# Undivided attention maps, moved sample steps, a written VectorE order in the projections and a shifted output end in a hybrid GLA and differential-attention step

## The chip, the cores and the metric

One core of one Trainium2 chip runs the whole step in a single launch. The metric is device time in microseconds (us) from the first to the last instruction and what lies around them. The times of before are 1455.91, 1458.81 and 1461.02 us; their median is 1458.81 us.

## The reference, cut to what matters

1024 prompt frames and 32 sample frames of width 1024 pass one layer: an input normalisation, one large input projection, a gated linear attention (GLA) branch, a differential attention branch, two output projections that are merged by sigmoid gates, an output projection with its own normalisation, and the residual. In the differential branch each head has two attention maps; they are subtracted, and the result is normalised per head and gated:

```python
p = jax.nn.softmax(s, axis=-1)
attn = p[:, :, 0] - lam * p[:, :, 1]
o = jnp.einsum('bhqk,bkhe->bqhe', attn, v.astype(F32))
...
yg = rmsnorm(o_gla, gla_norm_g) * silu(gg)
yd = rmsnorm(o_diff, diff_subln_g) * (1.0 - lambda_init) * silu(dg)
merged = sigmoid(ma) * (yg @ w_proj_gla) + sigmoid(mb) * (yd @ w_proj_diff)
return x + rmsnorm(merged @ w_out, post_norm_g)
```

where `rmsnorm(x, g)` is `x * rsqrt(mean(x * x) + EPS) * g`. The sample frames attend to 512 cached key and value rows and to themselves.

## The kernel before, in words

All matmuls run in float32 split into a high and a low part; a product takes three matmuls (high by high, high by low, low by high), and every split of a tile is a copy on ScalarE (ACT, the high part) and a difference on VectorE (DVE, the low part). TensorE is called PE, GpSimd POOL; SP issues most DMAs, in order.

The program has these stages, by the trace's time: normalisation and value projection to about 185 us; GLA to about 545; differential attention to about 1165; the GLA branch's output projection to about 1260; the other branch's projection to about 1360; the output projection in four quarters of 256 columns to 1448.4, and the end to 1458.4.

**The order on PE.** In the attention stage a planner, class `Order`, writes PE's order. Several threads yield steps, each with a cost, the events it needs with a latency behind each, and the PSUM banks it takes; the planner keeps a clock of its own and picks the first step that is ready. The latencies stand in table `W`. Wherever the attention thread is not ready, the thread `fill` puts in matmuls of the input projection (`ps_w`, L515 to L517). The order on DVE, ACT and POOL is left to the scheduler of the language there. The PSUM banks are two of 512 columns ("pj") and two of 1024 ("s"), one of 512 for transposes ("t") and one for outputs ("o").

**The attention stage.** For each of eight heads `diff_main` goes through eight blocks i of 128 queries. `diff_scores` computes both maps' scores (`ps_s`), their negative maxima (L941) and exponentials with row sums (L943); then the reciprocal of both sums (L946), the second map scaled by its reciprocal and minus lambda (L947, w columns wide), and the first map scaled and added to it (L948). `diff_main` transposes the result in fours into the t bank (`ps_t`, L997), splits it (L999, L1000), and multiplies it by the values (`po`). `split` leaves the rotated queries and keys of even heads in four parts of two early tiles, y2 and y3, of odd heads in tiles of their own; `load_y` fills the early tiles y0 to y3 with GLA outputs at the end of head 7 (L959 to L961).

**The sample heads.** `sample_thread` takes two heads at a time: scores against cache and new rows (`ps_ss`), softmax, transposes of the probabilities in two pieces (`ps_st`, 4 and 1 blocks of columns) each put together by ACT and DVE (L1073, L1074), the product with the values (`po_s`, L1084), a normalisation, and a transpose of the output (`ps_so`, L1095) into the t bank, read by two DVE instructions (L1098). The new value rows come into `vsm`, a part of tile `smp`.

**The projections.** `pg_first` runs GLA projection jobs 0 and 1 together, `pg_job` jobs 2 to 7; each has three chunks of 352 columns, 24 matmuls each, in two "pj" banks, and each chunk is evacuated by DVE (L1147). Beside them the eight attention outputs are loaded (`ydr`, L1130), multiplied on DVE by the inverse root of their mean square (`rsb`, L1206, two heads per load, one buffer), and split into `Y` (L1133, L1134). The next projection (L491 to L493) needs all eight. While a job runs, ACT and POOL split the next weights (L481, L483).

**The end.** For each quarter u of the columns and each of nine row blocks i (the ninth is the sample block) the product is squared and summed (L1270), scaled (L1271), and in the last quarter finished row block by row block: sum (L1276), inverse root (L183, and a power on POOL, L184), two halves of 512 columns scaled and added to the rows of x (L1279), and stored (L1281). The sample block is last in every quarter.

## Time and profile before

| | before |
|---|---|
| median of three runs | 1458.81 us |
| the profiled execution's own time | 1460.14 us |
| its span, first to last instruction | 1458.4 us |
| mean granted clock of TensorE | 0.991 |
| PE busy (matmul) | 1401.2 us, 96% |
| PE weight load, beside it | 1293.0 us, 89% |
| DVE busy | 748.8 us, 51% |
| ACT busy | 555.3 us, 38% |
| POOL busy | 297.9 us, 20% |

Busy times are summed over the instructions of an engine. The matmuls of a sequence overlap each other, so the difference between the span and PE's busy time, 57 us, is only roughly what PE waits; the waits are listed by instruction in a view of their own, and the granted clock is shown by slices of time.

### The profile page before, as it was taken

What the parts mean: (1) busy time and instruction counts of PE and PEld (TensorE: products, weight loads), DVE (VectorE), ACT (ScalarE), POOL (GpSimd) and SP (SyncE); (2) the same over time, 40 slices, a digit from 0 to 9 for tenths busy, and PEclk for the clock granted to TensorE, in tenths of its full rate; (3) what the DMA queues carried; (4) which work ended last, traced back from release to release, by engine and by line L of the source; (5) the groups of instructions that cost most, each with busy time, mean ns of one, the idle gap of its engine ahead of it and who ended that gap; (6) DMA issues with size and microseconds to landing.
All of it is one profiled execution on the core that took longest, in us unless ns stands there. A gap on an engine that the chain in (4) does not pass through costs nothing.

```text
span 1458.4 us, 22595 instructions
## 1 busy us (share of the span) xinstructions
PE 1401.2 (96%) x9072; PEld 1293.0 (89%) x9072; DVE 748.8 (51%) x1440; ACT 555.3 (38%) x1154; POOL 297.9 (20%) x194
## 2 busy tenths in 40 slices
PE   8999999999999999999999999999999999999997
PEld 6687789889989899998999898988888899999996
DVE  5622005656565342656575657656775425554425
ACT  4423104535354232545444444444444332221311
POOL 1200002222223123222222221222231112221001
PEclk9999999999999999999999999999999999999999
DMA  8522111122222233213122211221232188543416
GB/s 291 171 103 89 50 46 56 46 71 92 81 64 85 75 113 103 72 54 107 50 76 78 78 64 63 77 64 51 76 115 81 60 300 313 190 142 117 151 38 224
DMA packets 64803, 152.36 MB, mean 104 GB/s; under 512 B 9584, under 2 KB 28176, under 8 KB 63152
## 3 DMA queue, kind: packets, MB, share of 16 engines
q1 hardware_dynamic: 64688, 150.80, 31.2%
q8 instruction: 75, 1.23, 0.3%
q14 instruction: 40, 0.33, 0.1%
HBM read 108.57 MB, written 40.04 MB: 102 GB/s over the span
## 4 chain that ended last, share of the span: by engine, by line
PE 47%; DVE 9%; DMA 4%; ACT 3%; issue 2%; POOL 1%; SPq 0%; DVEq 0%; POOLq 0%; ACTq 0%
PE ps_w L515 9%; PE ps_w L516 8%; PE ps_w L517 8%; PE ps_s L937 4%; PE ps_t L997 2%; PE ps_w L492 2%; PE ps_w L491 2%; PE ps_w L493 2%; DVE nm L941 2%; DMA ydr<-ydd 1%; DMA cwr<-wout 1%; PE po L1011 1%; DVE p L947 1%; PE po L1012 1%; ACT p L943 1%
## 5 line engine op out<-in xcount | busy, mean ns | idle before, releaser
L515 PE MATMUL ps_w<-X,wh 128*128 128x352 f32 x1344 | 451.8, 336 | 2.3 <-DVE sg L530 1.6
L516 PE MATMUL ps_w<-X,wl 128*128 128x352 f32 x1344 | 436.8, 325 | 0.6 <-issue 0.6
L517 PE MATMUL ps_w<-X,wh 128*128 128x352 f32 x1344 | 434.8, 324 | 0.0
L483 POOL TENSOR_TENSOR wl<-wr,wh 128x1024 fp32r<-128x1024 f32 x72 | 176.1, 2446 | 624.2 <-ACT wh L481 548.7
L515 PEld LDWEIGHTS ps_w<-X,wh 128*128 128x128 f32 x1344 | 254.0, 189 | 9.9 <-issue 4.5
L516 PEld LDWEIGHTS ps_w<-X,wl 128*128 128x128 f32 x1344 | 254.5, 189 | 0.9 <-issue 0.9
L517 PEld LDWEIGHTS ps_w<-X,wh 128*128 128x128 f32 x1344 | 253.9, 189 | 0.0
L943 ACT ACTIVATE p<-ps_s,nm 128x256 f32<-128x256 f32 (+7 forms) x128 | 94.4, 740 | 70.7 <-DVE nm L941 70.4
L327 PE MATMUL ps_v<-wh,X 128*128 128x512 f32 x248 | 97.6, 394 | 1.8 <-DVE X L243 1.8
L326 PE MATMUL ps_v<-wh,X 128*128 128x512 f32 x248 | 99.1, 400 | 0.0
L328 PE MATMUL ps_v<-wl,X 128*128 128x512 f32 x248 | 98.4, 397 | 0.0
L481 ACT ACTIVATE wh<-wr 128x1024 fp32r<-128x1024 f32 x72 | 75.9, 1054 | 53.2 <-PE ps_w L517 30.3
L941 DVE TENSOR_REDUCE nm<-ps_s 128x1 f32<-128x256 f32 (+7 forms) x128 | 93.0, 752 | 0.0
L999 ACT ACTIVATE ah<-ps_t 128x512 fp32r<-128x512 f32 (+2 forms) x96 | 47.1, 490 | 70.3 <-PE ps_t L997 69.8
L1000 DVE TENSOR_TENSOR al<-ps_t,ah 128x512 fp32r<-128x512 f32 (+2 forms) x96 | 53.1, 553 | 25.4 <-ACT ah L999 24.3
L1015 DVE SCALAR_TENSOR_TENSOR osb<-po,gs_half,sg 128x256 f32<-128x256 f32 x32 | 15.4, 483 | 92.9 <-ACT sqo L1014 92.9
L492 PE MATMUL ps_w<-Y,wl 128*128 128x352 f32 x192 | 62.2, 324 | 0.0
L491 PE MATMUL ps_w<-Y,wh 128*128 128x352 f32 x192 | 62.0, 323 | 0.0
L493 PE MATMUL ps_w<-Y,wh 128*128 128x352 f32 x192 | 61.9, 322 | 0.0
L306 ACT ACTIVATE vo<-ps_v 128x512 f32<-128x512 f32 x32 | 19.1, 595 | 106.6 <-PE ps_v L328 106.1
L997 PE MATMUL ps_t<-ident,p 128*128 128x128 f32 x288 | 49.7, 282 | 9.8 <-DVE smp L1098 7.6
L327 PEld LDWEIGHTS ps_v<-wh,X 128*128 128x128 f32 x248 | 46.7, 188 | 13.6 <-DVE X L243 2.7
(316 smaller groups left out, 2713.9 us busy)
## 6 DMA issues: line engine op xcount, KB each, us to landing
wr<-w SPq DMA_DIRECT2D x72, 512.0 KB
thd<-gate SPq DMA_DIRECT2D x16, 528.0 KB
xn<-xn SPq DMA_DIRECT2D x16, 512.0 KB
wr<-wv SPq DMA_DIRECT2D x16, 512.0 KB
newk<-pair SPq DMA_DIRECT2D x8, 528.0 KB
y<-ygd SPq DMA_DIRECT2D x8, 528.0 KB
tha<-thd SPq DMA_DIRECT2D x8, 528.0 KB
ydr<-ydd SPq DMA_DIRECT2D x8, 528.0 KB
```

Source lines behind the costliest of these rows:

```text
L326: mm(ps, xk[:, 0, t0 : t0 + P], wh[:, k, :], start=(k == 0), stop=False)
L327: mm(ps, xk[:, 1, t0 : t0 + P], wh[:, k, :], start=False, stop=False)
L328: mm(ps, xk[:, 0, t0 : t0 + P], wl[:, k, :], start=False, stop=(k == KT - 1))
L483: nc.gpsimd.tensor_tensor(wl, wr, wh.bitcast(F32), op=ALU.subtract)
L491: mm(ps[:, :n], wh[:, k, :], src[k][:, 0, t0 : t0 + n], start=(k == 0), stop=False)
L492: mm(ps[:, :n], wl[:, k, :], src[k][:, 0, t0 : t0 + n], start=False, stop=False)
L493: mm(ps[:, :n], wh[:, k, :], src[k][:, 1, t0 : t0 + n], start=False, stop=(k == KT - 1))
L515: mm(ps[:, :n], wh[:, k, :], src[k][:, 0, t0 : t0 + n], start=(k == 0), stop=False)
L516: mm(ps[:, :n], wl[:, k, :], src[k][:, 0, t0 : t0 + n], start=False, stop=False)
L517: mm(ps[:, :n], wh[:, k, :], src[k][:, 1, t0 : t0 + n], start=False, stop=(k == KT - 1))
L941: ve.tensor_reduce(nm, ps[:, 0:w], axis=AX.X, op=ALU.max, negate=True)
L943: act(p[:, 0:w], ps[:, 0:w], AF.Exp, bias=nm, accum_out=sm[:, m : m + 1])
```

## The change

Five parts:

1. **Undivided maps.** The first map is no longer divided by its row sum. The sums of the first map go into 32 columns of `smp` (`den`, one column per head and block); the second map's reciprocal, times the first map's sum and minus lambda, is made on one column, and one instruction adds the second map, so scaled, to the first. The result is larger by the first map's sum, which the later normalisation takes out; for that, EPS is multiplied by the square of the sums: after heads 3 and 7 `den` is transposed (`ps_d`), squared on ACT with scale EPS, stored, and added to the mean squares before the root, which now works on 64 by 128 values.
2. **Early tiles.** The odd heads' splits take y2 and y3 instead of the even heads'; y0 and y1 are loaded first; the early tiles are split in three parts each.
3. **Sample heads.** New value rows are loaded with the keys; the output transpose takes the o bank; the planner's latencies `sp` and `so_t` are 8.6 instead of 7.1 and 2.9 instead of 0.72; the square's unused output goes elsewhere.
4. **Merge in fixed order.** The scaling and splitting of the attention outputs is called behind projection jobs 3 to 7, and DVE's order is as written there.
5. **Shifted end.** The sample block is taken last, fifth, fifth and second in the four quarters; the finishing of a row block is put behind the evacuation of the next one; the rows of x and the raw weights of the first quarter are loaded into other buffers; in the last quarter DVE's order is as written; the last half's store is issued by ACT.

The core of the diff:

```diff
-    "sp": 7.1, "st_t": 1.14, "sv": 3.44, "spt": 0.43, "so_o": 3.58, "so": 4.1, "so_t": 0.72, "yg0": 0.0,
+    "sp": 8.6, "st_t": 1.14, "sv": 3.44, "spt": 0.43, "so_o": 3.58, "so": 4.1, "so_t": 2.9, "yg0": 0.0,
...
-        hi, lo = (even[t] if h % 2 == 0 and t in even else dp.tile([P, NP], F32R, tag=f"{t}{h % 2}", name=t)
+        hi, lo = (odds[t] if h % 2 else dp.tile([P, NP], F32R, tag=f"{t}0", name=t)
...
-            act(p[:, 0:w], ps[:, 0:w], AF.Exp, bias=nm, accum_out=sm[:, m : m + 1])
+            act(p[:, 0:w], ps[:, 0:w], AF.Exp, bias=nm, accum_out=sums[m])
...
         ve.reciprocal(sm, sm)
-        ve.tensor_scalar(pt[1][:, 0:w], pt[1][:, 0:w], sm[:, 1:2], neglam, op0=ALU.mult, op1=ALU.mult)
-        ve.scalar_tensor_tensor(pt[0][:, 0:w], pt[0][:, 0:w], sm[:, 0:1], pt[1][:, 0:w], op0=ALU.mult, op1=ALU.add)
+        ve.tensor_scalar(sm, sm, sums[0], neglam, op0=ALU.mult, op1=ALU.mult)
+        ve.scalar_tensor_tensor(pt[0][:, 0:w], pt[1][:, 0:w], sm, pt[0][:, 0:w], op0=ALU.mult, op1=ALU.add)
...
+            if h % 4 == 3:
+                yield 0.1, [], ["t"]
+                pt = tbank("ps_d")
+                nc.tensor.transpose(pt[0 : 4 * NQ, 0:P], den, ident)
+                sq = tp.tile([4 * NQ, P], F32, tag="yt", name="sq")
+                act(sq, pt[0 : 4 * NQ, 0:P], AF.Square, scale=EPS ** 0.5)
+                S.free("t", W["m_o"])
+                st(sqd[(h - 3) * NQ : (h + 1) * NQ], sq)
...
             dma(kc, a["cachek"][h])
+            dma(vsm[0:NS, h % 2], a["newv"][NP:T, h * P : h * P + P])
...
-            yield 0.1, [(("so", h0), W["so"])], ["t"]
-            pt = tbank("ps_so")
+            yield 0.1, [(("so", h0), W["so"])], ["o"]
+            pt = obank("ps_so")
...
             def done():
                 st(ptd[j], tha[j])
                 load_tha(j + 2)
+                if j >= BESIDE[0]:
+                    for k in range(KT * (j - BESIDE[0]) // len(BESIDE), KT * (j + 1 - BESIDE[0]) // len(BESIDE)):
+                        split_yd(k)
...
+    def load_rsb(k):
+        if k < KT:
+            rsb[k // 2] = cp.tile([P, 2, NP], F32, tag="cwh", name="rsb")
+            dma(rsb[k // 2], rsd[k : k + 2, :].unsqueeze(0).to_broadcast([P, 2, NP]))
+
+    def split_yd(k):
+        r = ydr[k]
+        ve.tensor_tensor(r[:, 0:NP], r[:, 0:NP], rsb[k // 2][:, k % 2], op=ALU.mult)
+        act(yd[k][:, 0, :], r, AF.Copy)
+        ve.tensor_tensor(yd[k][:, 1, :], r, yd[k][:, 0, :].bitcast(F32), op=ALU.subtract)
+        if k % 2:
+            load_rsb(k + 1)
+        load_yd(k + 2)
...
+    with tc.manual_schedule(engines=PE | {mybir.EngineType.DVE}):
+        S.run(left)
...
+        if i == NQ - 1:
+            ends.pop(0)()
+        s1 = op.tile([P, 1], F32, tag="s1", bufs=2, name="s1")
+        ve.tensor_reduce(s1[0:w], ssq[0:w, i, :], axis=AX.X, op=ALU.add)
+        rsqrt_mean(s1, w, 1, D)
+        for e in ends:
+            e()
+        ends.clear()
...
+                ve.scalar_tensor_tensor(og[i][0:w, h], og[i][0:w, h], s1[0:w], xn[i][0:w, h], op0=ALU.mult, op1=ALU.add)
+                (nc.scalar.dma_start if i == NQ - 1 and lo else st)(a["y"][t0 : t0 + w, h], og[i][0:w, h])
...
+        at = (NQ, 4, 4, 1)[u]
+        with tc.manual_schedule(engines=PE | {mybir.EngineType.DVE}) if u == 3 else nullcontext():
+            for n, i in enumerate([*range(at), NQ, *range(at, NQ)]):
+                out_block(u, n, i, wh, wl, raw)
```

Here `BESIDE` is `range(3, KT)`, so split 0 is called behind job 3, splits 1 and 2 behind job 4, 3 behind job 5, 4 and 5 behind job 6, 6 and 7 behind job 7.

What this moves, at three places. First PE at the first pair of sample heads (`ps_st` are the transposed probabilities, `po_s` their product with the values, `ps_so` the transposed output, `ps_t` the prompt maps' transposes, `ps_w` fill). Before, the second `ps_st` and `po_s` stand here, and `ps_so` some 80 rows later, just ahead of a `ps_t`:

```order
L937 MATMUL ps_s<-kl,qh 128x128 x2
L937 MATMUL ps_s<-kh,ql 128x128 x2
L1071 MATMUL ps_st<-ident,p 32x128
L515 MATMUL ps_w<-X_85,wh 128x352
...
L517 MATMUL ps_w<-X_85,wh 128x352
L1084 MATMUL po_s<-vcs,smp 32x128 x8
L1084 MATMUL po_s<-smp 32x128 x2
L997 MATMUL ps_t<-ident,p 128x128 x4
...
L937 MATMUL ps_s<-kh,ql 128x384 x2
L1095 MATMUL ps_so<-ident,os__7332 128x64
L515 MATMUL ps_w<-X_85,wh 128x352
...
L997 MATMUL ps_t<-ident,p 128x128 x4
```

Of the change:

```order
L944 MATMUL ps_s<-pair 128x512 x6
L944 MATMUL ps_s<-pair 128x384 x6
L1088 MATMUL ps_st<-ident,p 32x128
L517 MATMUL ps_w<-X_84,wh 128x352
...
L519 MATMUL ps_w<-X_84,wh 128x352
L1101 MATMUL po_s<-vcs,smp 32x128 x8
L1101 MATMUL po_s<-smp 32x128 x2
L1006 MATMUL ps_t<-ident,p 128x128 x4
...
L1006 MATMUL ps_t<-ident,p 128x128 x2
...
L519 MATMUL ps_w<-X_84,wh 128x352
L1112 MATMUL ps_so<-ident,os__7494 128x64
L517 MATMUL ps_w<-X_85,wh 128x352
```

The second `ps_st` and `po_s` stand some 80 rows further on, behind a larger score group, and `ps_so` only four `ps_t` and two, and 24 fill matmuls, behind `po_s`.

Second, DVE in the GLA projection (`tha<-tha,ps_w` evacuates a chunk of PE's, `ydr<-ydr,rsb` is the multiplication, `Y<-ydr,Y` the difference). Before:

```order
L1147 SCALAR_TENSOR_TENSOR tha<-tha,ps_w 128x352 x9
L1206 TENSOR_TENSOR ydr<-ydr,rsb 128x1024 x2
L1134 TENSOR_TENSOR Y_13109<-ydr,Y_13109 128x1056
L1147 SCALAR_TENSOR_TENSOR tha<-tha,ps_w 128x352
L1134 TENSOR_TENSOR Y_13109<-ydr,Y_13109 128x1056
L1147 SCALAR_TENSOR_TENSOR tha<-tha,ps_w 128x352 x2
L1206 TENSOR_TENSOR ydr<-ydr,rsb 128x1024 x2
```

Of the change:

```order
L1155 SCALAR_TENSOR_TENSOR tha<-tha,ps_w 128x352 x12
L1229 TENSOR_TENSOR ydr<-ydr,rsb 128x1024
L1231 TENSOR_TENSOR Y_12709<-ydr,Y_12709 128x1056
L1155 SCALAR_TENSOR_TENSOR tha<-tha,ps_w 128x352 x3
L1229 TENSOR_TENSOR ydr<-ydr,rsb 128x1024
L1231 TENSOR_TENSOR Y_12709<-ydr,Y_12709 128x1056
L1229 TENSOR_TENSOR ydr<-ydr,rsb 128x1024
L1231 TENSOR_TENSOR Y_12709<-ydr,Y_12709 128x1056
L1155 SCALAR_TENSOR_TENSOR tha<-tha,ps_w 128x352 x3
```

Before, two multiplications followed each other and an evacuation stood between the two differences; now a whole split, or two, stands between the third evacuation of one job and the first of the next.

Third, DVE at the end (`sqj`'s sums are in `ssq`; `og...<-...,xn` are the halves that are finished). Before:

```order
L1271 TENSOR_TENSOR ogwwl_14008<-ps_c,gpost 128x256
L1276 TENSOR_REDUCE s_15038<-ssq 128x1
L183 TENSOR_SCALAR s_15038<-s_15038 128x1
L1279 SCALAR_TENSOR_TENSOR ogwwl_14008<-ogwwl_14008,s_15038,xn 128x512 x2
L283 TENSOR_TENSOR tl<-ps_c,tl 32x256 x3
L1271 TENSOR_TENSOR ogwwl_14009<-tl,gpost 32x256
L1276 TENSOR_REDUCE s_15065<-ssq 32x1
L183 TENSOR_SCALAR s_15065<-s_15065 32x1
L1279 SCALAR_TENSOR_TENSOR ogwwl_14009<-ogwwl_14009,s_15065,xn 32x512 x2
```

Of the change:

```order
L183 TENSOR_SCALAR s_15057<-s_15057 128x1
L1317 SCALAR_TENSOR_TENSOR ogwwh_14036<-ogwwh_14036,s_15019,xn 128x512 x2
L1301 TENSOR_TENSOR ogwwl_14038<-ps_c,gpost 128x256
L1317 SCALAR_TENSOR_TENSOR ogwwh_14037<-ogwwh_14037,s_15057,xn 128x512
L1308 TENSOR_REDUCE s_15095<-ssq 128x1
L183 TENSOR_SCALAR s_15095<-s_15095 128x1
L1317 SCALAR_TENSOR_TENSOR ogwwh_14037<-ogwwh_14037,s_15057,xn 128x512
L1317 SCALAR_TENSOR_TENSOR ogwwl_14038<-ogwwl_14038,s_15095,xn 128x512 x2
```

Before, the sample block (32 rows) was evacuated and finished behind the last full block; now the last full block's two halves are the last, with the half of the block ahead of it between.

## Rows read from the trace of the kernel before

**Rows 1.** Stage windows: us; PE, PEld, DVE, ACT, POOL busy; PEclk; DMA share; GB/s.

```profile
1165.00:1260.00 95.00, 93.91 (x580) 91.53 (x579) 43.25 (x48) 28.11 (x29) 18.18 (x8) 1.00 0.77 278
```

**Rows 2.** PE's waits, whole span: who waits for whom, us in total, times, longest.

```profile
PE ps_t L997 <- DVE smp L1098: 7.6, 4, 2.5
PE po_s L1084 <- DVE smp L1074: 3.4, 1, 3.4
...
PE ps_st L1071 <- DVE smp L1074: 3.0, 3, 1.7
PE ps_t L997 <- DVE p L948: 2.2, 2, 1.1
...
PE ps_c L278 <- DMA raw<-wout: 1.8, 1, 1.8
...
PE ps_w L515 <- DVE sg L530: 1.6, 1, 1.6
```

**Rows 3.** Windows of 10 us in the attention stage, same columns as Rows 1.

```profile
820.00:830.00 10.00, 9.50 (x66) 8.21 (x66) 6.06 (x15) 5.16 (x15) 0.55 (x1) 0.83 0.20 57
...
840.00:850.00 10.00, 8.66 (x62) 8.60 (x62) 4.19 (x8) 4.87 (x9) 0.49 (x1) 1.00 0.05 8
...
960.00:970.00 10.00, 6.39 (x56) 5.00 (x55) 9.66 (x20) 4.39 (x14) 1.81 (x1) 0.89 0.26 96
970.00:980.00 10.00, 10.00 (x60) 9.66 (x59) 2.83 (x8) 2.24 (x6) 0.54 (x1) 0.77 0.01 3
...
1130.00:1140.00 10.00, 7.50 (x42) 6.91 (x42) 7.69 (x12) 3.16 (x6) 1.04 (x1) 0.83 0.20 57
```

**Rows 4.** Timelines of the end: PE's last matmuls, ACT, and DVE.

```profile
1447.77 0.61 PE L278 MATMUL ps_c<-raw,mgs 128*32 128x256 f32 x8
...
1447.48 0.39 ACT L1270 ACTIVATE sqj<-ps_c 128x256 f32<-128x256 f32 x1 [2.25 <-PE ps_c L1262]
...
1448.66 0.42 DVE L1271 TENSOR_TENSOR ogwwl<-ps_c,gpost 128x256 f32<-128x256 f32 x1
...
1450.06 1.41 DVE L1279 SCALAR_TENSOR_TENSOR ogwwl<-ogwwl,s,xn 128x512 f32<-128x512 f32 x2 [0.73 <-POOL s L184]
...
1454.38 1.40 DVE L1279 SCALAR_TENSOR_TENSOR ogwwl<-ogwwl,s,xn 32x512 f32<-32x512 f32 x2 [0.72 <-POOL s L184]
```

**Rows 5.** Groups by line, shapes apart, DVE in the attention stage (545 to 1165).

```profile
L1000 DVE TENSOR_TENSOR al<-ps_t,ah 128x512 fp32r<-128x512 f32 x48 | 33.0, 687 | 16.0 <-ACT ah L999 15.3
...
L941 DVE TENSOR_REDUCE nm<-ps_s 128x1 f32<-128x896 f32 x16 | 16.7, 1085 | 0.0
```

**Rows 6.** Groups by line, DVE in the attention stage.

```profile
L947 DVE TENSOR_SCALAR p<-p,sm,neglam 128x128 f32<-128x128 f32 (+3 forms) x64 | 49.9, 779 | 1.8
...
L946 DVE RECIPROCAL sm<-sm 128x2 f32<-128x2 f32 x64 | 10.5, 165 | 53.2 <-ACT p L943 53.1
```

**Rows 7.** Timeline of DVE in the GLA projection.

```profile
1193.84 0.52 DVE L1147 SCALAR_TENSOR_TENSOR tha<-tha,ps_w 128x352 f32<-128x352 f32 x1 [2.93 <-PE ps_w L517]
1197.68 0.52 DVE L1147 SCALAR_TENSOR_TENSOR tha<-tha,ps_w 128x352 f32<-128x352 f32 x1 [3.33 <-PE ps_w L517]
...
1204.84 2.50 DVE L1206 TENSOR_TENSOR ydr<-ydr,rsb 128x1024 f32<-128x1024 f32 x2 [2.77 <-DMA rsb<-rsd]
...
1216.07 3.03 DVE L1206 TENSOR_TENSOR ydr<-ydr,rsb 128x1024 f32<-128x1024 f32 x2 [2.28 <-DMA ydr<-ydd]
```

**Rows 8.** One line's instructions, L1206: ns minimum, median, maximum.

```profile
L1206 DVE TENSOR_TENSOR ydr<-ydr,rsb x8: 1210/1292/2560, 1204.8 to 1241.4; 128x1024 f32<-128x1024 f32 x8
```

**Rows 9.** Groups by line, 1165 to 1260, ACT and DVE.

```profile
L1134 DVE TENSOR_TENSOR Y<-ydr,Y 128x1056 fp32r<-128x1056 f32 x8 | 10.0, 1255 | 0.1
...
L1133 ACT ACTIVATE Y<-ydr 128x1056 fp32r<-128x1056 f32 x8 | 8.7, 1089 | 14.6 <-DVE ydr L1206 14.4
```

**Rows 10.** Timeline of SP's issues in the GLA projection.

```profile
1196.62 0.38 SPq L1205 DMA_DIRECT2D rsb<-rsd  x1
...
1208.65 1.92 SPq L1130 DMA_DIRECT2D ydr<-ydd  x2
```

More of the change, by code (lines that the diff above doesn't have):

```diff
@@ L199, in hybrid_step_kernel @@
     rsd = dram.tile([DH, NP], F32, name="rsd")
+    sqd = dram.tile([DH * NQ, P], F32, name="sqd")
     def x_pair(name):
@@ L456, in hybrid_step_kernel @@
         ps = bank("ps_v")
[L457 removed]
+        sample_tiled(ps, xsw, [wrs[u][:, k, :] for k in range(KT)])
         value_tile(u, NQ, ps)
@@ L841, in hybrid_step_kernel @@
     qsam, ksam, sgs = {}, {}, {}
-    smp = tp.tile([P, 32, NS], F32, tag="b", name="smp")
+    smp = tp.tile([P, T], F32, tag="b", name="smp")
+    den = smp[:, NP:T]
+    smp = smp[:, 0:NP].rearrange("p (n t) -> p n t", t=NS)
     pT = smp[:, 0:10, :].rearrange("p (c h) t -> p c h t", h=2)
@@ L924, in diff_scores @@
         (qh, ql), (kh, kl) = dqs[h], dks[h]
-        sm = dp.tile([P, 2], F32, tag="sm", bufs=2, name="sm")
+        sm = dp.tile([P, 1], F32, tag="sm", bufs=2, name="sm")
+        n = h % 4 * NQ + i
+        sums = den[:, n : n + 1], sm
         pt = []
@@ L1100, in sample_thread @@
                 st(ydd[h, :, NP:T], y)
-            S.free("t", W["so_t"])
+            S.free("o", W["so_t"])
     jobs = []
@@ L1248, in hybrid_step_kernel, with out_block, half, finish @@
     ssq = op.tile([P, 9, 4], F32, name="ssq")
+    ends = []
+    def out_block(u, n, i, wh, wl, raw):
+        csl = slice(u * 256, u * 256 + 256)
+        w = P if i < NQ else NS
+        t0 = i * P
+        ps = (bank, dbank)[n % 2]("ps_c")[:, 0:256]
+        if i < NQ:
+            for k in range(KT):
+                mm(ps, mg[k][:, 0, t0 : t0 + P], wh[:, k, :], start=(k == 0), stop=False)
+                mm(ps, mg[k][:, 1, t0 : t0 + P], wh[:, k, :], start=False, stop=False)
+                mm(ps, mg[k][:, 0, t0 : t0 + P], wl[:, k, :], start=False, stop=(k == KT - 1))
+            src = ps
+        else:
+            sample_tiled(ps, mgs, raw)
+            src = op.tile([NS, 256], F32, tag="tl", name="tl")
+            sample_sum(src, ps)
+        sqj = op.tile([P, 256], F32, tag="sqj", name="sqj")
+        act(sqj[0:w], src[0:w], AF.Square, accum_out=ssq[0:w, i, u : u + 1])
+        ve.tensor_tensor(og[i][0:w, csl], src[0:w], gpost[0:w, csl], op=ALU.mult)
+        if u < 3:
+            return
+        if i == NQ - 1:
[6 more added lines that the diff above has]
+        ends.clear()
+        def half(lo):
+            def finish():
+                h = slice(lo, lo + 512)
+                ve.scalar_tensor_tensor(og[i][0:w, h], og[i][0:w, h], s1[0:w], xn[i][0:w, h], op0=ALU.mult, op1=ALU.add)
+                (nc.scalar.dma_start if i == NQ - 1 and lo else st)(a["y"][t0 : t0 + w, h], og[i][0:w, h])
+                if lo and i in later[:2]:
+                    load_rows(later[later.index(i) + 3])
+            return finish
+        ends.extend([half(0), half(512)])
+        if i == NQ - 1:
+            for e in ends:
+                e()
```

117 lines of the change are left out of this document (52 added, 65 removed).

## The prediction

> **What bounds the kernel now.** I read the busy times by stage first: TensorE (PE) is busy 93.9 of 95.0 us in the projection stage from 1165 on, VectorE (DVE) 43 [rows 1]; no stage has another engine near its limit. So an edit on DVE, ScalarE (ACT) or a DMA gains only what PE now waits, what PE loses at its lower clock, and what runs behind PE's last matmul; and it costs whenever it makes PE wait anew. Second, PE's waits [rows 2]: the attention stage has three of one kind. The transposes ps_t wait 7.6 us in four places for the two VectorE instructions that read the sample heads' transposed output; po_s waits 3.4 us and ps_st 3.0 us for the evacuation of the sample probabilities. There are also 2.2 us for scaled probabilities, 1.6 us for a gate, and 1.8 us for the raw output weights. Third, the granted clock in slices of 10 us [rows 3]: 0.83, 0.89, 0.77 and 0.83 in four slices, each at or behind one of these waits (PE is busy only 6.4 and 7.5 us in two of them). The matmuls ran partly at 1.2 instead of 2.4 GHz; what was lost is 10 us times 0.17, 0.11, 0.23 and 0.17, together 6.8 us. Last, the tail: PE ends at 1448.4, VectorE's last instruction starts at 1454.38, the span ends at 1458.4 [rows 4].
>
> The profiled run took 1460.14 us, span and surroundings; the median of the runs is 1.3 us lower. I sum against 1460.1 and then take 1.3 off. About 0.3% (4.4 us) is what a measurement of this kernel tells from no change.
>
> **The sample heads.** The transposed output ps_so moves from the t bank, where the next maps' transposes stood behind it, to the o bank; the whole wait of 7.6 us goes. The probabilities' second piece (ps_st) and po_s move some 13 us later in PE's order, each behind a score group, so the first piece has long been evacuated; these 6.4 us [rows 2] go mostly. What is late next: the second ps_st piece's evacuation now stands in VectorE's queue behind two score maxima of 896 columns, 1.09 us each [rows 5], while PE has six matmuls (1 us) between it and po_s. That leaves about 1.5 us for each of three of the four pairs, and 0.2 for the new ps_so, which comes only some 4 us after po_s: 5 us in all. The two latencies set (sp, so_t) act only through this order. The new value rows, two short loads on SP, now stand with the keys, a whole step before po_s reads them: 0. Net **-9** (bounds -14, if the maxima are done in time, and -6.5, if the three keep 2.5 us each, the longest of the ps_t waits [rows 2]). Along with the waits part of the clock loss goes: -4 of the 6.8 (bounds 0 and -6.8). I don't take it all, since waits of 1.5 us stay.
>
> **The undivided maps.** The scaling L947 of a whole map, 64 times, 49.9 us of VectorE, becomes one of a single column, like the reciprocal L946 at 0.165 us [rows 6]: some 39 us less. VectorE is not the bound there, so this is worth only the waits that name it: 2.2 us for p and 1.6 us for the gate (its VectorE queue shortens): **-3.8** (bound 0, if another wait ends last). New per half: one transpose of the sums, one square, one small store; they lie beside matmuls; the root over 64 x 128 instead of 8 x 1024 is read only behind job 3: 0. The last transposes of the last map now come as eight in a row, with no fill between. The t bank is one, so the second four wait for the first's copy on ACT and difference on VectorE, 0.69 us for the one [rows 5] and, as an estimate, as much for the other, plus hand-overs: **+1.6** (bound 0). The early tiles y0 and y1 load before y2 and y3 instead of behind: two loads move past each other on SP, 0, with bounds of 2.5 us either way, the longest of the ps_t waits [rows 2].
>
> **The projections.** This is where I see the cost. Before, VectorE's order was free: two multiplications in a row, and the evacuations of PE's chunks (L1147) slipped in between the differences. Now it is written out: behind jobs 3 to 7 each split (multiply, ACT copy, difference) comes whole, one or two of them between two jobs' evacuations. PE has two banks, and a chunk takes 3.84 us (the spacing of evacuations, 1193.84 and 1197.68) [rows 7], so it can go 7.7 us without an evacuation. Behind job 4 stand splits 1 and 2. Split 2 needs the second scale tile rsb, whose one buffer is free only when multiplication 1 is done; so its DMA is issued 0.52 + 1.21 us behind job 4's last matmul [rows 7, 8]. Then: DMA L, multiply 1.21, copy 1.09, difference 1.25, evacuation 0.52 [rows 7 to 9]. Job 5's first bank comes free at L + 5.8; the wait is L + 5.8 - 7.7. For L: the same 1 MB transfer was issued at 1196.62 and its multiplication began at 1204.84, after idling for it, 8.2 us; half the bytes, the second ydr, issued by 1210.57 (1208.65 + 1.92), took 5.5 us (1216.07) [rows 7, 10]. I take 8.2, the same transfer in the same stage: **+6.4** by 8.2 - 1.9 and a hand-over (lower bound 3.6).
>
> A rule of the Trainium skill speaks for less: its page "SBUF — State Buffer", section "The DMA setup-cost knee", fits a transfer as about 2 us and the bytes at 436 GB/s, by which 1 MB would land in 4.4 us (an estimate) and PE would wait 2.5 us. The rows disagree: 8.2 us for the same bytes [rows 7, 10].
>
> Behind jobs 6 and 7 again two splits: 0.52 + 2 x 3.55 + 0.52 = 8.1 us against 7.7, and GpSimd's weight split may hold up a VectorE instruction that starts beside it: L1206 takes up to 2.56 instead of 1.21 us [rows 8]. So 1.8 to 2 us for job 6 to 7; at the start of the next projection PE's order puts 46 matmuls (7.4 us, at 24 in 3.84) ahead of the one that needs the last difference, which is ready at 9.0 us with that hold-up, again about 2: **+4** (bounds 0 and 5). A PE wait of 6.4 us is longer than those behind which the clock fell [rows 2, 3]; those slices lost 1.7 to 3.4 us, so **+2.6** (bound 0).
>
> **The output stage.** The raw weights of the first quarter load earlier into other buffers: **-1.8** (bound 0). The row blocks' finishing is put behind the next block's evacuation, the rows of x are loaded ahead, and the sample block goes from the end to the second place. The tail of before held one full block and the sample block; now one full block: square 0.58, product 0.42, one half 0.7, reduce, scale and GpSimd's power 1.0 (two of about 0.16, like L946 [rows 6], and 0.73), two halves 1.4, and the last store's 2.6 (1455.78 to 1458.4) [rows 4], together 6.8 us against 10.0: **-3.2** (bounds -2.5, if one more half of 0.7 stands behind it, and -3.9, if one half less). The last half's store is issued from ACT, beside SP's; ACT has nothing behind it.
>
> **The sum.** -9 - 4 - 3.8 - 1.8 - 3.2 = -21.8; +1.6 + 6.4 + 4 + 2.6 = +14.6. Net -7.2, so 1452.9 on the profiled run and **1451.6** on the median.
>
> **Rivals.**
> 1. *The projection stage doesn't wait.* The second rsb is on time and VectorE is done early. Then 13.0 of the losses go: 1438.6. For: VectorE is busy under half of this stage. Against: the one buffer of rsb and 8.2 us in the row. 0.13.
> 2. *The transfer is quicker*, as the 5.5 us of the second ydr allow: the wait is 3.6 instead of 6.4 us, and the clock stays, as in 840 to 850, where PE idled 1.3 us at 1.00 [rows 3]. Then 2.8 + 2.6 = 5.4 less: 1446.2. For: the 8.2 us hold whatever was in flight ahead of rsb. Against: it is the only row of the same bytes. 0.12. The skill's fit above would make it 1445.
> 3. *Waits only move* (the change doesn't do what it says on PE). In the attention stage PE is fed by a planned order; it may wait as long at the moved po_s and ps_so: sample gain 6.5 instead of 9 and clock 0, 6.5 less: 1458; with the 3.8 gone too, 1462. For: the second ps_st evacuation stands behind two maxima. Against: the longest waits hang on the t bank. 0.22.
> 4. *Slower: the written order starves PE's banks.* At each of the three places (job 4 to 5, 6 to 7, start of the next projection) VectorE's multiplication is also held by GpSimd (1.35 us each), and behind each the clock falls as at 960 to 980 (3.4 us). Then 7.8 + 3.4 + 3.4 of waits and 10.2 of clock, 24.8 instead of 13.0: 1463.4; with the sample gain at its bound, 1466. It decides from about 25 us in this stage. For: each place has two banks and no cover. Against: only the first has a DMA in it. 0.15.
>
> My forecast, 1446 to 1457, has 0.38. **Range**: 1437 (rival 1, a little below) to 1465 (rival 3 and most of 4). Forecast and rivals 1 and 2 lie below 1454.4 (0.3% under the median) but for 0.05 of the forecast: faster 0.58. Within 0.3%: that 0.05 and most of rival 3, 0.23. Slower: rival 4 and the rest of 3, 0.19.
>
> **What would show it.** PE's waits after should have no ps_t for smp, and small ones at po_s; VectorE's one-column scaling should read about 0.15 us. Around job 5 in the projection PE should have one wait of 4 to 7 us that ends with VectorE's evacuation, with VectorE itself idle for rsb just before, and a clock under 1.00 behind it. The tail behind the last matmul should be near 6.8 us. If there is no wait at job 5, I was wrong on the DMA; if the attention stage is as long as before, on the moved waits.

## The result and the profile after

The changed kernel takes 1444.13 us (median of five runs, 1439.49 to 1445.76) against 1458.81 us: ratio 0.9904, 95% interval 0.9886 to 0.9922, some 14 us faster (14.7 between these medians). Forecast were 1451.6 us, 7.2 us faster, within 1437 to 1465. The direction was right, the size half. Run again later beside other variants (last group of experiments), the change had 0.9913 (0.9891 to 0.9936).

The profiled run of the change was its fastest, 1439.49 us at a mean clock of 0.998; the other four had 0.991 to 0.994. I therefore use two profiles of it, this one and that of the repetition (1443.11 us, clock 0.993), which stands nearer the median.

The page's busy line, where VectorE has lost 32 us and TensorE 7:

```profile
PE 1394.2 (97%) x9074; PEld 1288.8 (90%) x9074; DVE 717.0 (50%) x1448; ACT 556.6 (39%) x1164; POOL 299.9 (21%) x194
```

PE's waits in the change, whole span, to be read against [rows 2]:

```profile
PE ps_w L517 <- DVE tha L1155: 4.6, 2, 3.0
...
PE ps_t L1006 <- DVE smp L1091: 3.2, 3, 1.2
PE ps_t L1006 <- DVE al L1009: 2.3, 1, 2.3
...
PE po_s L1101 <- DVE smp L1091: 0.9, 3, 0.3
...
PE ps_w L495 <- DVE Y L1231: 0.7, 1, 0.7
...
PE ps_w L493 <- DVE thb L1250: 0.5, 1, 0.5
```

The waits for the sample heads have fallen from 14.0 to 4.1 us; those for p, the gate and the raw weights are gone. New are 4.6 us in two places of the GLA projection, 2.3 us at the last transposes of the attention, and 1.2 us at the start of the next projection.

The granted clock in windows of 10 us (us, PE busy, PEld, DVE, ACT, POOL, PEclk, DMA share, GB/s), first profile:

```profile
1130.00:1140.00 10.00, 7.72 (x53) 7.47 (x52) 5.41 (x11) 6.32 (x14) 2.37 (x1) 1.00 0.20 81
1140.00:1150.00 10.00, 10.00 (x72) 9.27 (x71) 2.44 (x3) 2.05 (x5) 0.00 (x0) 1.00 0.78 246
1210.00:1220.00 10.00, 7.33 (x37) 7.33 (x38) 3.78 (x5) 2.09 (x3) 0.64 (x1) 0.83 0.47 176
```

and of the repetition:

```profile
10.00:20.00 10.00, 7.70 (x21) 5.64 (x22) 7.15 (x15) 5.13 (x8) 1.46 (x1) 0.66 0.90 337
...
1140.00:1150.00 10.00, 9.27 (x60) 8.64 (x61) 1.85 (x3) 1.64 (x4) 1.93 (x1) 0.83 0.51 145
1210.00:1220.00 10.00, 7.02 (x37) 6.73 (x36) 3.82 (x5) 1.08 (x1) 0.00 (x0) 0.86 0.76 266
```

The four slices of before that were under full clock in the attention stage [rows 3] are gone in both. The wait of 2.3 us at the last transposes is there in both profiles, but only in the repetition does the clock fall behind it, to 0.83; there it reads:

```profile
1140.73 0.66 PE L1006 MATMUL ps_t<-ident,p 128*128 128x128 f32 x4 [2.27 <-DVE al L1009]
```

Behind the wait in the projection (it ends at 1212.67 and 1216.08) it fell in both. The slice at 10 us is at the start, where the change moves nothing, and the kernel before has it too (0.66).

By stages, in us, each from the first matmul of one stage to the first of the next (score, projection, output matmuls), the last one to the span's end:

| from to | before | change | change again | forecast | again less before |
|---|---|---|---|---|---|
| start to first scores | 587.7 | 584.8 | 586.9 | 0 | -0.8 |
| attention | 577.1 | 557.4 | 558.7 | -15.2 | -18.4 |
| GLA projection | 96.1 | 100.7 | 101.0 | | +4.9 |
| next projection | 92.6 | 94.9 | 94.9 | | +2.3 |
| both projections | 188.7 | 195.6 | 195.9 | +13.0 | +7.2 |
| output to end | 104.9 | 99.9 | 99.9 | -5.0 | -5.0 |

So the attention gained somewhat more than forecast, the projections lost about half of what was forecast, and the end came out as forecast. The total from the first scores on is -16.2 against a forecast of -7.2. (The profiles differ by 17.0 us, the medians by 14.7; a single pair of runs is good to 3 us or so.)

**Where the projections' loss is.** VectorE in the change behind job 4 (start us, duration, ..., idle before):

```profile
1201.97 0.52 DVE L1155 SCALAR_TENSOR_TENSOR tha<-tha,ps_w 128x352 f32<-128x352 f32 x1 [3.35 <-PE ps_w L519]
1202.41 1.22 DVE L1229 TENSOR_TENSOR ydr<-ydr,rsb 128x1024 f32<-128x1024 f32 x1
1204.78 2.23 DVE L1231 TENSOR_TENSOR Y<-ydr,Y 128x1056 fp32r<-128x1056 f32 x1 [1.16 <-ACT Y L1230]
1208.56 1.23 DVE L1229 TENSOR_TENSOR ydr<-ydr,rsb 128x1024 f32<-128x1024 f32 x1 [1.55 <-DMA rsb<-rsd]
1210.93 1.26 DVE L1231 TENSOR_TENSOR Y<-ydr,Y 128x1056 fp32r<-128x1056 f32 x1 [1.15 <-ACT Y L1230]
1212.11 0.95 DVE L1155 SCALAR_TENSOR_TENSOR tha<-tha,ps_w 128x352 f32<-128x352 f32 x2
```

and PE there:

```profile
1212.67 0.66 PE L517 MATMUL ps_w<-y,wh 128*128 128x352 f32 x1 [3.04 <-DVE tha L1155]
```

This is the chain of the prediction, step by step: evacuation, multiplication, difference, idle for rsb, multiplication, difference, evacuation, and PE waits for the last. Only the landing was shorter. The first of the two differences takes 2.23 us instead of 1.26; it began beside GpSimd's split of the next weights:

```profile
1203.16 2.73 POOL L485 TENSOR_TENSOR wl<-wr,wh 128x1024 fp32r<-128x1024 f32 x1 [8.83 <-ACT wh L483]
```

It ended 1.1 us behind that instruction (1207.01 and 1205.89). The five differences of these splits that began beside a weight split all took 2.2 to 2.3 us and ended 1.1 us behind it. SP's issues in the change:

```profile
1202.52 0.32 SPq L1188 DMA_DIRECT2D ptd<-tha  x1
1203.65 0.32 SPq L1225 DMA_DIRECT2D rsb<-rsd  x1
```

From 1203.65 to the multiplication at 1208.56 are 4.9 us, not 8.2. In the kernel before, two transfers had been issued just ahead of the one I had read:

```profile
1195.71 0.33 SPq L479 DMA_DIRECT2D wr<-w  x1
1196.14 0.38 SPq L1143 DMA_DIRECT2D tha<-thd  x1
```

two loads of 512 and 528 KB within the microsecond ahead of rsb; in the change it is one store of 528 KB. That this makes the difference was not tried by itself, and the other profiles bear it out only in part. Runs e3 to e6, e9 and e12, which keep this written order, have 4.4 to 5.1 us at this place. Run e1 has 8.6 us behind two loads and 8.1 us behind a load and a store, each pair issued within the microsecond ahead. But it has 7.4 us behind three loads issued within 1.4 us, and e7 has 7.7 us where the last transfer ahead was issued 2.9 us before.

The Trainium skill's fit ("SBUF — State Buffer", section "The DMA setup-cost knee": about 2 us and the bytes at 436 GB/s) gives 4.4 us for 1 MB, as an estimate. The 4.9 us of the change lie near it, the 8.2 us of before do not.

**Where the sample waits went.** VectorE and PE in the change at the first pair:

```profile
676.31 1.56 DVE L948 TENSOR_REDUCE nm<-ps_s 128x1 f32<-128x640 f32 x2
677.78 0.41 DVE L1091 TENSOR_TENSOR smp<-ps_st,smp 128x256 f32<-128x256 f32 x1
```

```profile
678.25 0.66 PE L1006 MATMUL ps_t<-ident,p 128*128 128x128 f32 x4 [1.22 <-DVE smp L1091]
```

An evacuation does stand behind two score maxima, but it is that of the first piece, and the one that waits is the next ps_t, for the t bank that this piece holds. At po_s only 0.3 us are left, in three of the four pairs.

**The end.** ACT and VectorE in the change:

```profile
1434.44 0.37 ACTq L1318 DMA_DIRECT2D y<-ogwwl  x1
```

```profile
1432.99 1.41 DVE L1317 SCALAR_TENSOR_TENSOR ogwwl<-ogwwl,s,xn 128x512 f32<-128x512 f32 x2 [0.44 <-POOL s L184]
```

The last half ends at 1434.40, the span at 1437.7: 3.3 us for a store of 128 rows, where before it was 2.6 us for one of 32 rows [rows 4]. PE's last matmul ended at 1429.95, so the tail is 7.8 us; forecast were 6.8. What the tail gave less, the output matmuls gave more: from their first to PE's end 94.9 us before and 92.1 now.

### The profile page after: what moved, and what is told of

Same layout as the page of the kernel before. It is cut to its first block, busy times and chain, and to the rows that moved or that the text cites. A ratio compares the mean times of both kernels' runs of the same rounds, so it can differ in the third digit from the quotient of the medians.

```text
span 1437.7 us, 22643 instructions
## 1 busy us (share of the span) xinstructions
PE 1394.2 (97%) x9074; PEld 1288.8 (90%) x9074; DVE 717.0 (50%) x1448; ACT 556.6 (39%) x1164; POOL 299.9 (21%) x194
## 4 chain that ended last, share of the span: by engine, by line
PE 58%; DVE 5%; ACT 1%; issue 1%; DMA 0%; POOLq 0%; DVEq 0%; ACTq 0%
PE ps_w L517 11%; PE ps_w L518 11%; PE ps_w L519 11%; PE ps_s L944 4%; PE ps_t L1006 2%; PE ps_c L1291 2%; PE ps_c L1293 2%; PE ps_c L1292 2%; PE ps_w L495 2%; PE ps_w L493 2%; PE ps_w L494 2%; PE po L1020 1%; PE po L1021 1%; DVE nm L948 1%; PE po L1019 1%
## 5 line engine op out<-in xcount | busy, mean ns | idle before, releaser
L328 PEld LDWEIGHTS ps_v<-wh,X 128*128 128x128 f32 x248 | 46.7, 188 | 12.7 <-issue 1.7
L329 PEld LDWEIGHTS ps_v<-wh,X 128*128 128x128 f32 x248 | 46.7, 188 | 12.5 <-DVE X L245 1.7
```

What stands on the lines that cost most here:

```text
L328: mm(ps, xk[:, 0, t0 : t0 + P], wh[:, k, :], start=(k == 0), stop=False)
L329: mm(ps, xk[:, 1, t0 : t0 + P], wh[:, k, :], start=False, stop=False)
```

## Experiments

Each ratio is to the kernel before on the same chip; the ratios are to be compared, since the medians of before ran from 1455.97 to 1458.81 us over the chips.

| run | median us | ratio to before | 95% interval |
|---|---|---|---|
| the change | 1444.13 | 0.9904 | 0.9886 to 0.9922 |
| e1 free order in the projection | 1439.94 | 0.9874 | 0.9860 to 0.9888 |
| e2 rsb as a ring | 1439.74 | 0.9870 | 0.9856 to 0.9885 |
| e3 maps divided | 1442.32 | 0.9889 | 0.9875 to 0.9904 |
| e4 sample part undone | 1456.40 | 0.9992 | 0.9982 to 1.0002 |
| e5 only the bank undone | 1454.43 | 0.9974 | 0.9961 to 0.9986 |
| e6 only sp undone | 1449.27 | 0.9939 | 0.9921 to 0.9958 |
| e7 before, sample part alone | 1440.83 | 0.9873 | 0.9853 to 0.9893 |
| e8 maps divided and ring | 1439.52 | 0.9870 | 0.9850 to 0.9890 |
| e9 the change again | 1444.26 | 0.9913 | 0.9891 to 0.9936 |
| e10 before, sample part and end | 1438.35 | 0.9871 | 0.9846 to 0.9895 |
| e11 before, undivided maps alone | 1447.47 | 0.9936 | 0.9913 to 0.9959 |
| e12 end undone | 1447.86 | 0.9939 | 0.9920 to 0.9958 |

### e1: VectorE's order free in the projection

```diff
-                if j >= BESIDE[0]:
...
-                        split_yd(k)
...
-    with tc.manual_schedule(engines=PE | {mybir.EngineType.DVE}):
-        S.run(left)
+    load_split(ydd, yd, lambda k: cp.tile([P, T], F32, tag=("cwr", "cwl")[k % 2], name="ydr"), scale)
```

Expected: 

> The changed kernel with its projection part undone: VectorE's order free again, the attention outputs scaled in pairs and split as before. Theory (the written order costs TensorE its banks, 4.6 + 0.7 us of waits and 1.7 us of clock in the changed kernel's trace): 4 to 7 us faster than the changed kernel, ratio to the kernel before about 0.986, and no wait of ps_w for tha over 0.6 us. Rival (the free order has its own waits, since the long multiplications then delay evacuations elsewhere, or the split stage ends later): within 2 us of the changed kernel, ratio 0.990.

Measured: 0.9874, 4.4 us less than the change, as the theory had it. But its reason fell:

```profile
PE ps_w L517 <- DVE tha L1164: 5.9, 6, 1.7
```

PE waits longer for these evacuations than in the change (5.9 against 4.6 us), in six places instead of two. What differs is the longest one, 1.7 instead of 3.0 us, and no slice under full clock follows any of the six. So the rival's mechanism is there as well. At one of the places a multiplication that began beside GpSimd's weight split (at 1196.17) takes 3.45 us, the evacuation stands behind it, and PE waits 1.6 us for that:

```profile
1196.35 3.45 DVE L1226 TENSOR_TENSOR ydr<-ydr,rsb 128x1024 f32<-128x1024 f32 x1
```

In the profiles the two projections take 194.4 us (195.9 in the repetition of the change), 1.5 us less. This gain is not at job 5: the GLA projection takes 101.8 us, 0.8 more than in the repetition, and the next projection has the 92.6 us of before again, 2.3 less. The mean clock of the runs is higher, 0.995 against 0.994 and 0.993 in the two groups of the change, which over the span is worth 2 to 4 us; the clock behind the wait at job 5 is in both figures, so they can't be added.

Against the kernel before, the free order does not bring the GLA projection back: 101.8 against 96.1 us. There PE waited for these evacuations only

```profile
PE ps_w L515 <- DVE tha L1147: 0.5, 2, 0.3
```

So what the written order costs is 1.5 us in the profiles and 4.4 us between the medians. The rest of the projections' loss of 7 us does not come back with the order free, and which part of the change brings it is not shown.

### e2: the scale tile as a ring

```diff
-            rsb[k // 2] = cp.tile([P, 2, NP], F32, tag="cwh", name="rsb")
-            dma(rsb[k // 2], rsd[k : k + 2, :].unsqueeze(0).to_broadcast([P, 2, NP]))
+            if not rsb:
+                rsb[0] = cp.tile([P, 2, NP], F32, tag="cwh", name="rsb")
+            dma(rsb[0][:, k % 2], rsd[k : k + 1, :].to_broadcast([P, NP]))
...
-        if k % 2:
-            load_rsb(k + 1)
+        load_rsb(k + 2)
```

Expected: 

> The changed kernel, but the scale tile rsb is loaded head by head into two halves of the same tile, each two heads ahead, so that no multiplication waits for its load. Theory (the wait behind job 4 is the one buffer of rsb): the 1.55 us in which VectorE idles for rsb go, the 3.0 us wait of ps_w at job 5 falls to about 1.6 us, what job 7 has, and the clock drop behind it goes: 1.5 to 3 us faster than the changed kernel. Rival (the two whole splits between evacuations make the wait, whatever rsb does): under 0.5 us faster, the job 5 wait stays near 3 us.

Measured: 0.9870, 5 us less than the change, more than the 1.5 to 3 expected. PE's waits there:

```profile
PE ps_w L517 <- DVE tha L1155: 2.8, 2, 1.4
```

VectorE no longer idles for rsb, the wait at job 5 has fallen from 3.0 to 1.4 us, what job 7 has, and 1210 to 1220 runs at full clock. Both projections take 192.6 us, 3.3 less than in the repetition: 1.6 of the wait and 1.7 of the clock. The other 2 us of the medians' difference I can't place. That VectorE's wait for rsb, which had one buffer, makes the long wait is shown; the edit also halves each load, and these two were not parted.

The fall of the clock is less sure than the wait. In e5, which keeps the one buffer, PE waits at the same place even a little longer (the longest of these two waits, it ends at 1227.68), and no slice behind it is under full clock:

```profile
PE ps_w L517 <- DVE tha L1155: 4.7, 2, 3.2
```

```profile
1220.00:1230.00 10.00, 6.80 (x42) 6.51 (x42) 5.20 (x5) 1.08 (x1) 0.74 (x1) 1.00 0.85 303
1230.00:1240.00 10.00, 10.00 (x64) 10.00 (x63) 4.77 (x5) 2.15 (x2) 2.76 (x1) 1.00 0.65 224
```

### e3: maps divided

The edit takes back the one-column scaling, the sums in `smp` and the later EPS term:

```diff
-        ve.tensor_scalar(sm, sm, sums[0], neglam, op0=ALU.mult, op1=ALU.mult)
-        ve.scalar_tensor_tensor(pt[0][:, 0:w], pt[1][:, 0:w], sm, pt[0][:, 0:w], op0=ALU.mult, op1=ALU.add)
+        ve.tensor_scalar(pt[1][:, 0:w], pt[1][:, 0:w], sm[:, 1:2], neglam, op0=ALU.mult, op1=ALU.mult)
+        ve.scalar_tensor_tensor(pt[0][:, 0:w], pt[0][:, 0:w], sm[:, 0:1], pt[1][:, 0:w], op0=ALU.mult, op1=ALU.add)
```

Expected: 

> The changed kernel with the maps divided as before: the second map scaled over its whole width on VectorE, the sums' transposes and squares left out. Theory (VectorE is not the bound; only 3.8 us of TensorE waits named it): 2 to 5 us slower than the changed kernel, ratio about 0.993. Rival (in the attention stage 40 us less on VectorE lets every evacuation come earlier, and the greater part of the 20 us gained there is its): 8 to 15 us slower, ratio 0.996 to 1.000.

Measured: 0.9889. Both theories miss: dividing again costs nothing; if anything it is 2 us faster, but the intervals overlap. The 2.3 us wait at the last transposes becomes 0.9, and the waits of ps_t for the samples rise from 3.2 to 4.0:

```profile
PE ps_t L1005 <- DVE smp L1082: 4.0, 3, 1.5
...
PE ps_t L1005 <- DVE al L1008: 0.9, 1, 0.9
```

With the sample steps moved, the undivided maps save nothing that PE waits for.

### e4 to e6: the sample part, and its two halves

e4 undoes all of it; e5 undoes the bank (and so_t, which belongs to it); e6 undoes the latency sp alone:

```diff
-            yield 0.1, [(("so", h0), W["so"])], ["o"]
-            pt = obank("ps_so")
+            yield 0.1, [(("so", h0), W["so"])], ["t"]
+            pt = tbank("ps_so")
```

```diff
-    "sp": 8.6, "st_t": 1.14, "sv": 3.44, "spt": 0.43, "so_o": 3.58, "so": 4.1, "so_t": 2.9, "yg0": 0.0,
+    "sp": 7.1, "st_t": 1.14, "sv": 3.44, "spt": 0.43, "so_o": 3.58, "so": 4.1, "so_t": 2.9, "yg0": 0.0,
```

Expected of e4: 

> The changed kernel with the sample heads as before: output transpose in the t bank, both latencies and the loading of the new value rows as they were. Theory (the sample waits and the clock behind them are the greater part of the gain): the ps_t waits for the sample outputs come back with 5 to 8 us, po_s and ps_st with 3 to 6, and clock 2 to 7: 10 to 16 us slower than the changed kernel, ratio 0.997 to 1.001. Rival (with a shorter VectorE queue these waits are short anyway): 2 to 6 us slower, ratio 0.992 to 0.995.

Expected of e5: 

> The changed kernel with the sample heads' output transpose back in the t bank and so_t back at 0.72; sp stays 8.6 and the new value rows come with the keys. The run with all of the sample part undone was 12 to 13 us slower than the changed kernel. Theory (the bank is the greater half, as its four waits of 7.6 us were in the kernel before): the ps_t waits for the sample outputs come back with 5 to 8 us and two clock drops with them: 7 to 10 us slower than the changed kernel, ratio 0.995 to 0.998. Rival (the latency is it: the early second ps_st and po_s made the long waits and the clock drops): under 4 us slower, ratio 0.990 to 0.993.

Expected of e6: 

> The changed kernel with only the planner's latency sp back at 7.1, so that the second ps_st and po_s stand early again behind a small score group; the output transpose keeps the o bank and so_t 2.9. Theory (bank is the greater half): ps_st and po_s waits of 3 to 6 us come back, with one or two clock drops: 4 to 7 us slower than the changed kernel, ratio 0.993 to 0.996. Rival (the latency is all of it): 9 us or more slower, ratio from 0.997.

Measured: e4 0.9992, 12.8 us slower than the change; e5 0.9974, 10 us slower; e6 0.9939, 5 us slower. In time the theory holds in all three. In the waits it holds nearly: po_s and ps_st come back with 6.5 us, for 3 to 6 expected, and in e5 the waits for the samples come back in other places. PE's waits in e4:

```profile
PE ps_t L1006 <- DVE smp L1115: 6.5, 4, 1.8
...
PE po_s L1101 <- DVE smp L1091: 4.2, 2, 3.4
...
PE ps_st L1088 <- DVE smp L1091: 2.3, 2, 1.4
```

in e5:

```profile
PE ps_so L1112 <- DVE al L1009: 4.2, 2, 4.0
PE ps_t L1006 <- DVE smp L1091: 3.6, 2, 2.4
...
PE ps_t L1006 <- ACT qh L886: 2.7, 1, 2.7
```

and in e6:

```profile
PE po_s L1101 <- DVE smp L1091: 4.2, 2, 3.4
...
PE ps_st L1088 <- DVE smp L1091: 2.3, 2, 1.4
```

The two kinds of [rows 2] come back with their edit: sp brings back the waits of po_s and ps_st to the tenth of a microsecond that e4 has. The bank brings the ps_t waits back in e4; in e5 the planner puts ps_so elsewhere, where ps_so itself waits 4.0 us for the bank. The slices under full clock come back too; in the attention stage e4 has three (0.66, 0.83, 0.83), e5 three and e6 three, the change's first profile none. In e4 the attention takes 571.8 us, 14.4 more than in the change's first profile; named waits make 9 of it, slices under full clock 6.8 (10 times 0.34, 0.17 and 0.17), and part of such a slice lies in a wait.

### e7, e11: each of the two attention parts alone, on the kernel before

e7 has these lines (and the new value rows loaded with the keys, the square's output elsewhere):

```diff
-    "sp": 7.1, "st_t": 1.14, "sv": 3.44, "spt": 0.43, "so_o": 3.58, "so": 4.1, "so_t": 0.72, "yg0": 0.0,
+    "sp": 8.6, "st_t": 1.14, "sv": 3.44, "spt": 0.43, "so_o": 3.58, "so": 4.1, "so_t": 2.9, "yg0": 0.0,
...
-            pt = tbank("ps_so")
+            pt = obank("ps_so")
...
-            S.free("t", W["so_t"])
+            S.free("o", W["so_t"])
```

e11 has these, with the sums' transposes and the new root:

```diff
-        ve.tensor_scalar(pt[1][:, 0:w], pt[1][:, 0:w], sm[:, 1:2], neglam, op0=ALU.mult, op1=ALU.mult)
+        ve.tensor_scalar(sm, sm, sums[0], neglam, op0=ALU.mult, op1=ALU.mult)
```

Expected of e7: 

> The kernel before with only the sample part of the change (bank, both latencies, new value rows with the keys). Theory (the sample part is nearly all of the gain, and the rest of the change cancels to little): ratio to the kernel before 0.989 to 0.993, that is 10 to 16 us faster. Rival (it pays only with the shorter VectorE queue of the undivided maps): ratio 0.995 or more, with ps_t or po_s waits for the sample probabilities of over 4 us in all.

Expected of e11: 

> The kernel before with the undivided maps alone. Prediction on record for this part: 3.8 us less for waits that name VectorE, 1.6 us more for the last transposes. Theory now (VectorE's 32 us less shift the scheduler's order but end no wait that matters): within 3 us of the kernel before, ratio 0.998 to 1.002, while VectorE's busy time falls by some 30 us. Rival (with the old sample order the shorter VectorE queue shortens the sample waits too): ratio 0.993 to 0.997.

Measured: the sample part alone 0.9873, 18 us faster than before and 4 us faster than the whole change; the maps alone 0.9936, 9 us faster, where I had forecast 2.2 and then expected nothing. PE's waits with the maps alone:

```profile
PE ps_t L1003 <- DVE smp L1112: 6.5, 4, 1.8
PE po_s L1098 <- DVE smp L1088: 4.2, 2, 3.4
...
PE ps_st L1085 <- DVE smp L1088: 2.3, 2, 1.4
```

with the sample part alone:

```profile
PE ps_t L997 <- DVE smp L1074: 4.0, 3, 1.5
...
PE po_s L1084 <- DVE smp L1074: 0.9, 3, 0.3
```

The maps leave the sample waits nearly as they were (13.0 against 14.0 us). What they end in this profile are slices under full clock: one is left in the attention stage (0.83 at 960) instead of four, 5.1 us less loss, and the small waits for p and the gate, 3.8 us. Together 8.9, and the measured gain is 9.3. But that is one profile: over all runs the mean clock was 0.9943 with the maps alone and 0.9926 before on the same chip, which is worth only some 2 us of clock, so the 5.1 us are not shown for the other runs. The sample part ends the same slices, and in its profile the wait for p is down to 0.7 us without the maps. So, as far as a profile of each shows, the two parts reach for the same losses: either pays alone, and with the sample part in, the maps have nothing left (e3).

### e8: both of e3 and e2

The edits are the two diffs above, in one kernel.

Expected: 

> The changed kernel with the divided maps of before and the scale tile as a ring of two halves: both edits that cost nothing or gained by themselves (ratios 0.9889 and 0.9870 against the kernel before). Theory (they act at different places): 4 to 6 us faster than the changed kernel, ratio 0.985 to 0.987. Rival (both remove the same clock drop at job 5, so the gains don't add): as the ring alone, ratio 0.987 to 0.989.

Measured: 0.9870, as the ring alone. It lies on the border of both ranges, so this run can't part theory from rival; it shows no gain beyond the ring's.

### e9, e10, e12: the change again, the best of the parts, the end

e9 has no edit. e10 is e7 with the change's output stage, e12 the change with that of before; the core of e10's second edit, which e12 turns round:

```diff
-        for i in range(NQ + 1):
+            for n, i in enumerate([*range(at), NQ, *range(at, NQ)]):
...
-                xn = op.tile([P, D], F32, tag="xn", bufs=3, name="xn")
-                dma(xn[0:w], a["xn"][t0 : t0 + w, :])
...
+        ends.extend([half(0), half(512)])
```

Expected of e9: 

> The changed kernel itself once more, beside the others of this chip. Its profiled run was the fastest of five, with one slice of 10 us under full clock (1210 to 1220); the other four took 4 to 6 us more at a mean clock of 0.991 to 0.994. Theory (the PE waits at the end of the attention stage, 2.3 us, and at job 5, 3.0 us, cost a clock drop in most runs, besides the wait): median 1442 to 1446, and a profile with two to four such slices, among them one at 1140 or 1210 to 1230. Rival (the five runs were drawn badly; the kernel takes what the variants with one part undone take): median 1439 to 1441.

Expected of e10: 

> The kernel before with the sample part and the shifted output end alone; maps, early tiles and projections as before. Theory (sample part and end are all that pays: the end gave 3.0 us less from the first output matmul to the last instruction, 99.9 against 102.9 us): 2.5 to 4 us faster than the sample part alone, ratio to the kernel before 0.984 to 0.986, the fastest of all. Rival (the end's gain is eaten by run to run changes of the clock): within 1 us of the sample part alone, 0.987.

Expected of e12: 

> The changed kernel with the output stage as before: sample block last, finishing at once, rows of x loaded late. Prediction on record for this part: 1.8 us for the raw weights and 3.2 us for the tail. Theory: 3 to 5 us slower than the changed kernel beside it, the tail behind the last matmul 10 us instead of 8. Rival (only the tail counts, 2 us): 1 to 2.5 us slower.

e9 came out at 1444.26 us, as its theory had it; its slices under full clock lie at 1140 and 1210, as expected, behind the waits named there. e12, the output stage of before put back into the change, is 3.6 us slower than the change beside it, as its theory had it, though the two intervals overlap; the raw weights' wait is back:

```profile
PE ps_c L280 <- DMA raw<-wout: 2.7, 1, 2.7
```

and from the first output matmul to the end it takes 106.1 us instead of 99.9, 1.7 of them in two slices under full clock behind that wait (0.95 and 0.88, from 1360 on); the tail is 9.7 us, for 7.8 in the change. e10, the kernel before with only the sample part and the new end, is the fastest kernel by its median, 1438.35 us, and 6 us faster than the change on the same chip. Against the sample part alone (0.9873) its ratio of 0.9871 tells no difference; the 2.5 to 4 us expected did not come and the rival holds, though the profile has the shorter end (100.4 us from the first output matmul against 102.9). In its profile no slice between 30 and 1420 us is under full clock:

```profile
1130.00:1140.00 10.00, 10.00 (x68) 9.96 (x67) 5.74 (x9) 4.54 (x9) 0.00 (x0) 1.00 0.04 16
1140.00:1150.00 10.00, 9.54 (x71) 8.58 (x70) 2.37 (x4) 4.01 (x7) 2.42 (x1) 1.00 0.62 219
1210.00:1220.00 10.00, 10.00 (x63) 9.82 (x62) 5.08 (x8) 3.23 (x3) 1.65 (x1) 1.00 0.93 346
```

e1, e2, e7, e8 and e10 are not told apart by their intervals. All have a lower ratio than the change (the intervals of e7, e8 and e10 overlap with it a little), and all lack the one long wait at job 5: none waits over 1.7 us for an evacuation there.

## Why the prediction was right, and where its sizes were off

- **The bound and the kind of gain**: right. TensorE is busy 97% now, and every microsecond gained or lost that I could place is a wait of it, a slice under full clock, or the tail.
- **The sample heads, -9 and -4 of clock**: right, and the greatest part. The waits fell by 9.9 us. The undone part costs 12.8 us (e4). The remaining wait, forecast at po_s behind the second piece's evacuation, stands at ps_t behind the first piece's; its size, 4.1 against 5 us, fits, its place was wrong. In the attention stage the clock gave more: all four slices, 6.8 us, are gone in both profiles of the change, where I took 4; the one at 1140 in the repetition belongs to the last transposes. Over the whole span this is not left: the mean clock was 0.9925 in the six later runs of the change and 0.9926 in the runs of before beside them, and slices behind the new waits stand where those of before are gone. Forecast for the clock was -4 and +2.6.
- **The maps, -3.8 and +1.6**: the waits named are gone, and the last transposes wait 2.3 us, for 1.6 forecast; but alone the maps are worth 9 us and in the change nothing (e11, e3). I had priced the parts as if they could be added, and the clock loss only with the sample part. That the attention as a whole still came near its forecast (-18.4 for -15.2) is in part luck. I also took the one-column scaling for 0.165 us; it takes more:

```profile
L955 DVE TENSOR_SCALAR sm<-sm,smp,neglam x64: 265/272/276, 586.9 to 1131.0; 128x1 f32<-128x1 f32 x64
```

- **The projections, +6.4 + 4 + 2.6**: this is the term that did most to make the forecast half of the result. The long wait and its cause are shown (e2), but each size was too high: the wait at job 5 is 3.0 us for 6.4, because I took a landing of 8.2 us that had two other loads ahead of it; with the 4.9 us that it took, the prediction's own formula, L + 5.8 - 7.7, gives 3.0. Job 7 waits 1.5 for 2, the next projection 1.2 for 2. The difference that takes 2.23 us beside GpSimd's weight split (1.26 otherwise) falls into the time in which rsb is on its way, so it costs nothing at job 5. The clock falls behind the wait at job 5, 1.7 us for 2.6. Waits and clock make 7.4 us, for 13.0. The reading that the order makes the whole loss is not borne out: with the order free the GLA projection waits 5.9 us for evacuations (e1), and only 1.5 us of the two projections' time come back. Of the rivals, the quicker transfer (1446.2 us) came nearest to the result.
- **The output stage, -1.8 and -3.2**: the sum is right (5.0 us less in the profiles; 3.6 us by e12, between medians). The tail is 7.8 us, not 6.8: I used a store of 32 rows for one of 128 (2.6 against 3.3 us), and reduction, scale and power took 1.4 us, not 1.0.
- **Open**: e4 has the maps and the end, which alone and beside the change are worth 9 and 3.6 us, but is only 1 us faster than the kernel before. Against the maps alone its profile is 6.9 us longer in the projections (198.0 against 191.1) and 5.4 us longer in the attention stage (571.8 against 566.4), where the written order does not act; its runs have a lower clock (0.988 to 0.993 against 0.993 to 0.997). At 1083 PE waits 2.1 us in e4 and 0.9 us with the maps alone, and a slice under full clock follows only in e4. At 1125 the waits are alike, 1.8 us in both, and still the clock falls in e4 alone. The early tiles are in e4 and not in the other, but were not undone by themselves, so their part is not known.

## What to carry to other kernels

Where one engine bounds the whole span, price each part of a change by the waits it ends, and look whether another part ends the same ones: here two parts were worth 18 and 9 us alone, and the change, which has both, gained no more than the first. One long wait can cost twice, by itself and by the clock behind it; cutting the one of 3.0 us to 1.4 (by a second half of a buffer) gave 3.3 us in the profiles and some 5 between the medians. A landing time read from a trace may hold only with the transfers that were ahead of it: look at what its queue had just issued. To say what an order costs, free it in the changed kernel and compare with the kernel before as well: here the free order had waits of its own.
